# Neighbourhood attention in an encoder: left and right key blocks folded into one before exp and transposes, scores three steps ahead, bias table built in other places

## The chip, the cores and the metric

The kernel runs on one core of a Trainium2 chip. The metric is the device time of one execution in microseconds (us). Times of runs are medians of several executions; a trace is one profiled execution, which has a time of its own. PE is the matrix engine (TensorE), PEld its weight loads, DVE VectorE, ACT ScalarE, POOL GpSimd, SP the engine whose queue issues the DMAs here.

## What is computed

The program is an encoder of two layers on 1024 tokens (a grid of 16 rows by 64 columns) of width 1024, in fp32. Layer 0 has mixer A, attention of 16 heads of width 64 over a window of 8 rows by 16 columns; layer 1 has mixer B, attention over all keys. Each is followed by an output projection and a gated embedding. The change touches mixer A alone:

```python
rs = np.clip(r - win_r // 2, 0, rows - win_r)
cs = np.clip(c - win_c // 2, 0, GRID_W - win_c)
...
sc = jnp.einsum('bhqd,bhqnd->bhqn', qb, kg).astype(jnp.float32) * scale
sc = sc + bb.astype(jnp.float32)[None]
pr = jax.nn.softmax(sc, axis=-1).astype(vg.dtype)
return jnp.einsum('bhqn,bhqnd->bhqd', pr, vg)
```

`bb` is a learned bias for each head and each row and column offset. The result is multiplied by silu(gate) and projected.

## The kernel before

**Tiles.** The tokens are put in another order first: each of the 8 tiles of 128 tokens holds all 16 rows of 8 neighbouring columns. A window of 16 columns then lies in a query's own tile and the two beside it (`near(j)`), so a query block j has scores for 3 key blocks (2 at the edges, j = 0 and 7). Of the left block a query at column c of its tile sees the keys with column at least c, of the right block those with column below c; the two sets complement each other. A mask of a large number (`MK`) takes out the rest.

**Number format.** Matmuls take every fp32 operand as a high part (an ACT copy in fp32r) and a low part (a DVE subtraction of it), so a product is 2 or 3 matmuls on line 303.

**A step.** The loop runs over 16 heads h and 8 blocks j, 128 steps n. With the sign of the scores turned, step (h, j) issues, in the order of the code:

- `head`: due work of the list `later` (among it `fin`, the gating of a finished pair of heads), and at j = 1 `table(h + 1)`: one DMA of the next head's bias (`u`, line 609, SP) and five POOL subtractions of 128x128 (line 612) that make `tb` = mask minus bias.
- `f_T(h, j)`: one PE transpose for each key block (line 654), then the ACT copy PTh (657) and the DVE subtraction PTl (658). There are two PSUM buffers `t`.
- `f_E` of step n + 1: ACT's exp (646) over all blocks, with the row's minimum `mn` as bias, and row sums.
- `f_S` of step n + 2: two matmuls into `s`, then one DVE instruction (637) that adds `tb`, writes `sp` to SBUF and takes the minimum. `sp` and `mn` have three buffers.
- `f_AV` of step n - 2: the products with V, key block by key block, from PTh and PTl.

**Dense work.** `mix` spreads matmuls of the projections (q and k of head h + 1, gates, for h = 3, 7, 11 also V of the next four heads) between these pieces in proportion to weights. Every fourth head, 3, 7 and 11, therefore takes longer. Each engine executes its instructions in the order in which they were issued, one queue for each.

**The end of a pair of heads.** `head_end` (line 418) sends reciprocals of the row sums over DRAM by SP (`r8T` to `rD`, line 436, `rD` to `rb`, 438). `fin`, four ticks later, has two POOL products of 128x512, Y by G (499) and Y by rb (500). Eleven pulses later ACT makes the high part (496, written to `rb`), DVE the low part (497), and SP stores both (492).

**Weights.** They come through a staging buffer (`wstage`, SP) and are split by ACT and DVE (lines 218 and 219) between the other work. q and k of a head are split on DVE by lines 588, 589, 590 and 593, four times two for each head.

Of the kernel before, what the change touches and what calls it, by code (L numbers as in the profile page):

```python
# [11 lines left out]
F32 = mybir.dt.float32  # L12
F32R = mybir.dt.float32r
# [70 lines left out]
def lay_out(inp):  # L84
# [46 lines left out]
    ok = np.stack([rowok, left, rowok, right, rowok], axis=1)  # L131
    mask = np.where(ok, 0.0, BIG).astype(np.float32)

    inv = np.power(np.float32(10000.0), -np.arange(16, dtype=np.float32) * np.float32(2.0) / np.float32(32.0)).astype(np.float32)
# [7 lines left out]
    def swap(v):  # L142
# [5 lines left out]
        "x": tokens(g["x"][0]), "wts": W, "rpb": rpb, "gains": gains, "hgains": hg,  # L148
        "mask": mask, "rope": np.stack([cosT, sinT], axis=1),
    }  # L150


@with_exitstack
def trunk(ctx, tc, x, wts, rpb, gains, hgains, mask, rope, out):
    nc = tc.nc
# [384 lines left out]
    def mixer_a():  # L540
        with ExitStack() as es:
# [64 lines left out]

            def table(h):
                u = sb.tile([128, 16, 24], F32, name="u", bufs=1)
                sync.dma_start(u, U2[h].rearrange("p (r c) -> p r c", r=16))
                tb = sb.tile([128, 640], F32, name="tb").rearrange("p (k c) -> p k c", k=5)  # L610
                for k, c0 in ((0, 0), (1, 0), (2, 8), (3, 16), (4, 16)):
# [3 lines left out]
                TB[h] = tb  # L615

# [3 lines left out]
            def f_S(h, j):  # L620
                k0, k1 = near(j)
                n = (k1 - k0 + 1) * 128
                ps = psS.tile([128, 512], F32, name="s")
                qt = QS[h][:, j * 128:(j + 1) * 128]
                ks = slice(k0 * 128, (k1 + 1) * 128)
                mm(ps[:, :n], qt, KA[h][:, ks], True, False)
                mm(ps[:, :n], qt, KB[h][:, ks], False, True)
                if j == 0:
                    RS[h] = sb.tile([128, 8], F32, name="rs", bufs=3)
                    tb = TB[h][:, 2:5:2]  # L630
                elif j == NT - 1:
                    tb = TB[h][:, 0:3:2]
                else:
                    tb = TB[h][:, 1:4]
# [12 lines left out]

            def f_T(h, j):
                k0, k1 = near(j)
                m = k1 - k0 + 1  # L650
                sp, _ = SP.pop((h, j))
                ps = psT.tile([128, 4, 128], F32, name="t")
                for i in range(m):
                    pe.transpose(ps[:, i], sp[:, i * 128:(i + 1) * 128], ident)  # L654
                f0 = k0 * 3 + (j - k0 + 1)
                sl = slice(f0, f0 + 2 * m - 1, 2)
# [6 lines left out]
            def f_AV(h, kb):  # L663
# [3 lines left out]
                for hf in range(2):  # L667
                    a, b = max(j0, 4 * hf), min(j1, 4 * hf + 3)
                    if a > b:
                        continue  # L670
                    first = OP[h][hf] is None
                    if first:
                        OP[h][hf] = psO.tile([128, 512], F32, name="o")
                    o = OP[h][hf][:, (a - 4 * hf) * 128:(b + 1 - 4 * hf) * 128]
                    s0 = kb * 3 + a - kb + 1
                    sl = slice(s0, s0 + b - a + 1)
                    last = kb == (4 if hf == 0 else 7)
                    mm(o, V[:, kb, h % 4], PTh[:, sl], first, False)
                    mm(o, V[:, kb, h % 4], PTl[:, sl], False, last)
# [65 lines left out]
            vs[0][1]()  # L745
            sync.dma_start(MK, mask)
            for c in range(8):
                sync.dma_start(U[:, c], rpb[:, :, 7 - c:31 - c])
            for t in range(1, NT):
# [8 lines left out]
                vs[t][1]()  # L758
                if t == 6:
                    table(0)  # L760
                WQ.pump(t > 2)
# [7 lines left out]
            ptp = es.enter_context(tc.tile_pool(name="ptp", bufs=1))  # L769
            PTh = ptp.tile([128, NT * 3, 128], F32R, name="PTh")  # L770
            PTl = ptp.tile([128, NT * 3, 128], F32R, name="PTl")
            for d in qk_items(0):
# [9 lines left out]
            f_E(0, 0)  # L782
            f_S(0, 1)
            steps = [(h, j) for h in range(NH) for j in range(NT)]

# [6 lines left out]
            for h in range(NH):  # L792
                att = []
                for j in range(NT):
                    n = h * NT + j
                    def head(h=h, j=j):
                        later.tick()
                        if j == 1 and h + 1 < NH:
                            table(h + 1)
                    att.append((head, CA[0]))  # L800
                    att.append((lambda h=h, j=j: f_T(h, j), CA[1]))
                    if n + 1 < len(steps):
                        att.append((lambda n=n: f_E(*steps[n + 1]), CA[2]))
# [9 lines left out]
                if h == NH - 1:  # L813
                    att += [(lambda: f_AV(NH - 1, NT - 2), CA[4]), (lambda: f_AV(NH - 1, NT - 1), CA[4])]
                dense = []
# [469 lines left out]

NAMES = ["x", "wts", "rpb", "gains", "hgains", "mask", "rope"]

# [14 lines left out]
```

## Time and profile before

| what | value |
| --- | --- |
| median of 3 runs | 1562.63 us (1560.91 to 1562.86) |
| the profiled execution | 1564.6 us |
| span of its trace | 1562.8 us |
| PE busy, whole span | 1520.8 us (97%) |
| DVE, ACT, POOL busy | 965.3, 871.6 and 320.3 us |
| mixer A, 60 to 545 us of the trace: PE, DVE, ACT, POOL busy | 476.11, 298.78, 282.17 and 77.67 us |

The span is the trace's own measure; the 1.8 us between it and the time of the execution lie outside it. An engine's busy time is summed over instructions; on PE, matmuls overlap, so that one instruction's duration is longer than the distance from its start to that of the next.

### The profile page before, as it was taken

To read this page: it belongs to the slowest core of one execution; us is meant where nothing else is said; L and a number is where in the kernel's file an instruction comes from. 1 tells how busy PE (TensorE), PEld (TensorE's weight loads), DVE (VectorE), ACT (ScalarE), POOL (GpSimd) and SP (SyncE) were. 2 spreads that over 40 slices of the span, in tenths; PEclk is the share of its full clock that TensorE was granted. 3 is DMA by queue.
4 is the path that set the end of the run, shared out by engine and by line. 5 is a ranking of instruction groups with operands and counts; after the bars stand their busy time and mean duration, and the time that the engine had idled before them with its cause. 6 is when DMAs were issued, how large, how long until landed. Compare 5 with 4: busy or idle time off the path is not lost.

```text
span 1562.8 us, 23940 instructions
## 1 busy us (share of the span) xinstructions
PE 1520.8 (97%) x9048; PEld 1328.0 (85%) x9048; DVE 965.3 (62%) x1660; ACT 871.6 (56%) x1744; POOL 320.3 (20%) x409
## 2 busy tenths in 40 slices
PE   6999999999999999999999999999999999999998
PEld 6888988988988788888988889989899888778886
DVE  5566576476467434536767776677777777624533
ACT  6565465466366523433566776776767777622422
POOL 3102102112012010000433142553141400000124
PEclk9999999999999999999999999999999999999999
DMA  8211222132122962132210111101101213651113
GB/s 288 83 40 53 66 67 78 40 93 79 40 80 83 340 237 90 53 130 104 77 49 22 38 51 42 59 24 55 50 27 46 77 39 107 233 202 54 68 59 130
DMA packets 89859, 138.82 MB, mean 89 GB/s; under 512 B 16913, under 2 KB 55953, under 8 KB 89745
## 3 DMA queue, kind: packets, MB, share of 16 engines
q1 hardware_dynamic: 85136, 122.62, 23.9%
q10 hardware_dynamic: 4608, 14.68, 2.6%
q8 instruction: 71, 1.16, 0.3%
q14 instruction: 44, 0.35, 0.1%
HBM read 104.65 MB, written 36.15 MB: 90 GB/s over the span
## 4 chain that ended last, share of the span: by engine, by line
PE 81%; ACT 6%; DVE 6%; issue 3%; POOL 2%; DMA 2%; SPq 0%; ACTq 0%; POOLq 0%; DVEq 0%
PE d L303 54%; PE o L303 10%; PE s L303 8%; PE t L1057 6%; PE t L654 2%; DVE PTl L1060 2%; PE t L413 2%; DVE mn L1041 1%; DMA wstage<-in_wts 1%; ACT PTh L1059 1%; ACT wh L218 1%; ACT P L1047 1%; POOL xn L402 1%; DVE wl L219 1%; POOL tb L612 1%
## 5 line engine op out<-in xcount | busy, mean ns | idle before, releaser
L303 PE MATMUL d<-wh,HTh 128*128 128x256 f32 (+1 forms) x1096 | 372.3, 340 | 4.9 <-ACT HTh L414 2.6
L303 PE MATMUL d<-wh,HTl 128*128 128x256 f32 (+1 forms) x1096 | 365.7, 334 | 1.5 <-DVE HTl L415 1.5
L303 PE MATMUL d<-wl,HTh 128*128 128x256 f32 (+1 forms) x1096 | 365.2, 333 | 0.0
L1060 DVE TENSOR_TENSOR PTl<-t,PTh 128x512 fp32r<-128x512 f32 x256 | 164.4, 684 | 123.4 <-ACT PTh L1059 122.8
L303 PEld LDWEIGHTS d<-wh,HTh 128*128 128x128 f32 x1096 | 207.7, 189 | 28.4 <-ACT HTh L414 3.2
L303 PEld LDWEIGHTS d<-wh,HTl 128*128 128x128 f32 x1096 | 207.7, 189 | 23.8 <-DVE HTl L415 2.1
L303 PEld LDWEIGHTS d<-wl,HTh 128*128 128x128 f32 x1096 | 208.0, 190 | 21.4
L303 PE MATMUL d<-HTh,wh 128*128 128x512 f32 x504 | 206.1, 409 | 0.0
L303 PE MATMUL d<-HTl,wh 128*128 128x512 f32 x504 | 197.7, 392 | 0.0
L303 PE MATMUL d<-HTh,wl 128*128 128x512 f32 x504 | 197.7, 392 | 0.0
L1047 ACT ACTIVATE P<-s,mn 128x1024 f32<-128x1024 f32 x128 | 142.8, 1115 | 58.3 <-DVE mn L1041 57.7
L1059 ACT ACTIVATE PTh<-t 128x512 fp32r<-128x512 f32 x256 | 139.9, 594 | 43.2 <-PE t L1057 42.3
L1041 DVE TENSOR_REDUCE mn<-s 128x1 f32<-128x1024 f32 x128 | 154.7, 1209 | 11.7 <-PE s L303 11.5
L1057 PE MATMUL t<-ident,P 128*128 128x128 f32 x1024 | 137.4, 275 | 6.7 <-DVE PTl L1060 4.8
L219 DVE TENSOR_TENSOR wl<-wstage,wh 128x1024 fp32r<-128x1024 f32 x89 | 113.8, 1284 | 39.9 <-ACT wh L218 39.4
L1057 PEld LDWEIGHTS t<-ident,P 128*128 128x128 f32 x1024 | 114.7, 141 | 22.5 <-DVE PTl L1060 16.5
L303 PE MATMUL s<-KA,QS 128*128 128x512 f32 (+2 forms) x384 | 133.7, 402 | 0.0
L303 PE MATMUL o<-PTh,V 128*128 128x256 f32 (+2 forms) x672 | 119.0, 288 | 3.3 <-ACT PTh L657 1.7
L303 PE MATMUL s<-KB,QS 128*128 128x512 f32 (+2 forms) x384 | 121.8, 371 | 0.0
L303 PE MATMUL o<-PTl,V 128*128 128x256 f32 (+2 forms) x672 | 119.5, 289 | 0.4 <-DVE PTl L658 0.3
L658 DVE TENSOR_TENSOR PTl<-t,PTh 128x384 fp32r<-128x384 f32 (+1 forms) x128 | 66.6, 520 | 79.3 <-ACT PTh L657 78.3
L303 PEld LDWEIGHTS d<-HTh,wl 128*128 128x128 f32 x504 | 94.6, 188 | 22.0
(159 smaller groups left out, 2456.7 us busy)
## 6 DMA issues: line engine op xcount, KB each, us to landing
wstage<-in_wts SPq DMA_DIRECT2D x92, 512.0 KB
X<-in_x SPq DMA_DIRECT2D x16, 512.0 KB
pp<-ppD SPq DMA_DIRECT2D x32, 256.0 KB
rb<-rD SPq DMA_DIRECT2D x56, 128.0 KB
ppD<-th SPq DMA_DIRECT2D x24, 256.0 KB
xD<-X SPq DMA_DIRECT2D x8, 512.0 KB
X<-xD SPq DMA_DIRECT2D x8, 512.0 KB
yD0h<-rb SPq DMA_DIRECT2D x14, 256.0 KB
```

Source lines behind the costliest of these rows:

```text
L218: act.activation(hi, s, AF.Copy)
L219: self.rest = lambda: dve.tensor_tensor(lo, s, hi, ALU.subtract)
L303: pe.matmul(ps, a, b, start=first, stop=last, skip_group_check=True)
L402: pool.tensor_scalar(xns[i][:, :512], xts[i][:, :512], r[:, i:i + 1], None, op0=ALU.mult)
L413: pe.transpose(ps[:, k], xn[:, (4 * c + k) * 128:(4 * c + k + 1) * 128], ident)
L654: pe.transpose(ps[:, i], sp[:, i * 128:(i + 1) * 128], ident)
L658: dve.tensor_tensor(PTl[:, sl], ps[:, :m], PTh[:, sl], ALU.subtract)
L1041: dve.tensor_reduce(mn, ps, axis=AX.X, op=ALU.min)
L1047: act.activation(p, ps, AF.Exp, bias=mn, scale=-1.0, accum_out=RS[h, hf][:, t:t + 1])
L1057: pe.transpose(ps[:, i], p[:, k * 128:(k + 1) * 128], ident)
L1059: act.activation(PTh[:, ks, c], ps, AF.Copy)
L1060: dve.tensor_tensor(PTl[:, ks, c], ps, PTh[:, ks, c], ALU.subtract)
```

## The change

Before, a step has 3 blocks at exp and at the transposes. After, DVE takes the element-wise minimum of the left and the right block behind the wide score instruction (for j = 1 to 6, so 6 times for each of 16 heads, 96 in all), and exp, transposes, PTh and PTl handle 2 blocks. Since each element is masked in one of the two blocks, the minimum is the one that isn't. Behind the transposes two POOL instructions of 128x2x128 pull the two apart again with a mask RI: right = folded by RI, left = folded minus right. PTh and PTl are now the two halves of one tile PT. The scores are still computed at 3 blocks, and the products with V are the same in number and width.

The scores run three steps ahead (four buffers of `sp` and `mn`), the products with V three steps behind. The bias of head h + 1 is fetched at j = 0, and its table is built at j = 2 (two blocks) and j = 3 (three), where all of it stood at j = 1. For head 0 the opening loop over tiles fetches the bias at t = 5 and builds the table at t = 7, where both stood at t = 6. The mask RI is a new input of 64 KB, loaded once behind MK.

```diff
+            RI = one.tile([128, 128], F32, name="RI")
...
-            def table(h):
+            def bias(h):
                 u = sb.tile([128, 16, 24], F32, name="u", bufs=1)
                 sync.dma_start(u, U2[h].rearrange("p (r c) -> p r c", r=16))
...
+            def table(h, ks):
...
-                sp = sb.tile([128, 384], F32, name="sp", bufs=3)
-                mn = sb.tile([128, 1], F32, name="mn", bufs=3)
+                sp = sb.tile([128, 384], F32, name="sp", bufs=4)
+                mn = sb.tile([128, 1], F32, name="mn", bufs=4)
...
+                if n == 384:
+                    dve.tensor_tensor(sp[:, 0:128], sp[:, 0:128], sp[:, 256:384], ALU.min)
...
                 n = (k1 - k0 + 1) * 128
+                n = min(n, 256)
                 sp, mn = SP[h, j]
...
-                for i in range(m):
+                for i in range(2):
                     pe.transpose(ps[:, i], sp[:, i * 128:(i + 1) * 128], ident)
...
-                act.activation(PTh[:, sl], ps[:, :m], AF.Copy)
-                dve.tensor_tensor(PTl[:, sl], ps[:, :m], PTh[:, sl], ALU.subtract)
+                act.activation(PT[:, 0, sl], ps[:, :2], AF.Copy)
+                dve.tensor_tensor(PT[:, 1, sl], ps[:, :2], PT[:, 0, sl], ALU.subtract)
+                if m == 3:
+                    left, right = PT[:, :, f0], PT[:, :, f0 + 4]
+                    pool.tensor_tensor(right, left, RI[:, None].to_broadcast([128, 2, 128]), ALU.mult)
+                    pool.tensor_tensor(left, left, right, ALU.subtract)
...
-                        if j == 1 and h + 1 < NH:
-                            table(h + 1)
+                        if h + 1 < NH:
+                            if j == 0:
+                                bias(h + 1)
+                            elif j == 2:
+                                table(h + 1, (2, 4))
+                            elif j == 3:
+                                table(h + 1, (0, 1, 3))
...
-                    if n + 2 < len(steps):
-                        att.append((lambda n=n: f_S(*steps[n + 2]), CA[3]))
-                    if n >= 2:
-                        att += av_and_v(*steps[n - 2])
+                    if n + 3 < len(steps):
+                        att.append((lambda n=n: f_S(*steps[n + 3]), CA[3]))
+                    if n >= 3:
+                        att += av_and_v(*steps[n - 3])
```

In the changed kernel the lines that the next listings name have these numbers: 620 is the table's subtraction, 500 and 501 are the products Y by G and Y by rb, 672 and 673 the two that pull the blocks apart; on ACT 657 is exp, 668 the copy PT, 497 the high part of Y, 583, 586 and 587 the copies of a projection of q and k, 219 the high part of weights; on SP 611 is the bias, 204 the staging of weights, 437 and 439 the two legs of the row sums.

**POOL, around the first finished pair (head 2).** Before:

```order
L612 TENSOR_TENSOR tb<-MK,u 128x128 x20
L499 TENSOR_TENSOR Y<-Y,G 128x512
L500 TENSOR_TENSOR Y<-Y,rb 128x512
L499 TENSOR_TENSOR Y<-Y,G 128x512
L500 TENSOR_TENSOR Y<-Y,rb 128x512
L612 TENSOR_TENSOR tb<-MK,u 128x128 x10
```

After:

```order
L620 TENSOR_TENSOR tb<-MK,u 128x128 x2
L672 TENSOR_TENSOR PT<-PT,RI 128x2x128
L673 TENSOR_TENSOR PT<-PT 128x2x128
L500 TENSOR_TENSOR Y<-Y,G 128x512
L501 TENSOR_TENSOR Y<-Y,rb 128x512
L620 TENSOR_TENSOR tb<-MK,u 128x128 x3
```

The table of head 3 stood whole ahead of the first pair's two products; now two of its five blocks and a step's pulling apart stand ahead of them, and the other three behind.

**ACT, head 2, around the high part of that pair's Y.** Before:

```order
L584 ACTIVATE QS<-th 64x512
L585 ACTIVATE KA<-th 64x512
L657 ACTIVATE PTh<-t 128x3x128
L646 ACTIVATE sp,rs<-sp,mn 128x384
L496 ACTIVATE rb<-Y 128x512
L657 ACTIVATE PTh<-t 128x3x128
L646 ACTIVATE sp,rs<-sp,mn 128x384
```

After:

```order
L657 ACTIVATE sp,rs<-sp,mn 128x256
L583 ACTIVATE th<-d 128x512
L219 ACTIVATE wh_1358<-wstage 128x1024
L497 ACTIVATE rb<-Y 128x512
L586 ACTIVATE QS<-th 64x512
L587 ACTIVATE KA<-th 64x512
L668 ACTIVATE PT<-t 128x2x128
```

The high part of Y stood ahead of the copy of step (2, 4) and now stands one step later, ahead of the copy of step (2, 5).

**SP, head 2.** Before:

```order
L436 DMA rD<-r8T 8x32 x4
L438 DMA rb<-rD 64x512 x2
L203 DMA wstage<-in_wts 128x1024
L609 DMA u<-U_84 128x384
L436 DMA rD<-r8T 8x32 x4
```

After:

```order
L611 DMA u<-U_84 128x384
L204 DMA wstage<-in_wts 128x1024
L437 DMA rD<-r8T 8x32 x4
L439 DMA rb<-rD 64x512 x2
L437 DMA rD<-r8T 8x32 x4
```

The bias of head 3 stood behind the first pair's first row sums and a weight tile and now stands ahead of both.

## Rows read from the trace of the kernel before

**Rows 1.** The page, busy time of each engine over the whole span (share, instructions):

```profile
PE 1520.8 (97%) x9048; PEld 1328.0 (85%) x9048; DVE 965.3 (62%) x1660; ACT 871.6 (56%) x1744; POOL 320.3 (20%) x409
```

**Rows 2.** Windows: length, busy PE, PEld, DVE, ACT, POOL (instructions), clock, DMA share, GB/s:

```profile
60.00:545.00 485.00, 476.11 (x2704) 414.08 (x2704) 298.78 (x675) 282.17 (x626) 77.67 (x103) 1.00 0.27 88
...
84.24:134.85 50.61, 49.32 (x262) 41.89 (x262) 36.21 (x85) 32.69 (x73) 8.79 (x9) 1.00 0.21 68
```

**Rows 3.** Timeline of PE: start, duration, line, operation; three transposes, then a step with two:

```profile
96.22 0.39 PE L303 MATMUL d<-HTh,wl 128*128 128x512 f32 x1
96.45 0.49 PE L654 MATMUL t<-ident,sp 128*128 128x128 f32 x3
...
96.95 0.34 PE L303 MATMUL s<-KB,QS 128*128 128x384 f32 x1
...
134.85 0.38 PE L654 MATMUL t<-ident,sp 128*128 128x128 f32 x2
...
135.24 0.34 PE L303 MATMUL s<-KB,QS 128*128 128x384 f32 x1
```

**Rows 4.** Groups by form, mixer A: count | busy us, mean ns of one | idle before:

```profile
L654 PE MATMUL t<-ident,sp 128*128 128x128 f32 x352 | 60.4, 275 | 6.0 <-ACT sp L646 5.6
L646 ACT ACTIVATE sp<-sp,mn 128x384 f32<-128x384 f32 x96 | 58.9, 614 | 11.1 <-DVE mn L637 10.5
L658 DVE TENSOR_TENSOR PTl<-t,PTh 128x384 fp32r<-128x384 f32 x96 | 53.4, 556 | 66.2 <-ACT PTh L657 65.3
L657 ACT ACTIVATE PTh<-t 128x384 fp32r<-128x384 f32 x96 | 47.1, 490 | 51.0 <-PE t L654 49.6 <-issue 0.8
L588 DVE SCALAR_TENSOR_TENSOR QS<-th,QS 64x512 fp32r<-64x512 f32 x32 | 23.4, 731 | 7.2 <-ACT QS L584 6.3
L646 ACT ACTIVATE sp<-sp,mn 128x256 f32<-128x256 f32 x32 | 16.2, 505 | 2.8 <-DVE mn L637 2.8
L658 DVE TENSOR_TENSOR PTl<-t,PTh 128x256 fp32r<-128x256 f32 x32 | 13.2, 412 | 13.1 <-ACT PTh L657 13.0
L657 ACT ACTIVATE PTh<-t 128x256 fp32r<-128x256 f32 x32 | 12.3, 383 | 11.3 <-PE t L654 10.5
```

**Rows 5.** Groups by form, mixer B: SBUF operations of two inputs on POOL and DVE:

```profile
L878 POOL TENSOR_TENSOR qt<-qt,t 128x256 f32<-128x256 f32 x24 | 19.4, 807 | 1.9
...
L878 DVE TENSOR_TENSOR qt<-qt,t 128x128 f32<-128x128 f32 x8 | 2.4, 302 | 0.3
```

**Rows 6.** Waits: who waited on whom, total us, times, median us:

```profile
ACT rb L496 <- POOL Y L500: 11.8, 3, 4.3
...
PE t L654 <- ACT sp L646: 5.6, 6, 1.5
```

**Rows 7.** Timeline, SP, POOL, ACT and PE in heads 2 and 14:

```profile
113.10 0.37 SPq L609 DMA_DIRECT2D u<-U  x1
...
117.14 3.06 POOL L612 TENSOR_TENSOR tb<-MK,u 128x128 f32<-128x128 f32 x5 [35.14 <-DMA u<-U]
...
123.17 0.63 ACT L496 ACTIVATE rb<-Y 128x512 fp32r<-128x512 f32 x1 [4.10 <-POOL Y L500]
...
124.83 0.55 PE L654 MATMUL t<-ident,sp 128*128 128x128 f32 x3 [1.29 <-ACT sp L646]
...
492.58 0.61 ACT L646 ACTIVATE sp<-sp,mn 128x384 f32<-128x384 f32 x1 [3.46 <-DVE mn L637]
...
493.34 0.55 PE L654 MATMUL t<-ident,sp 128*128 128x128 f32 x3 [1.27 <-ACT sp L646]
```

**Rows 8.** Two DVE lines, ns min/median/max, first to last start:

```profile
L588 DVE SCALAR_TENSOR_TENSOR QS<-th,QS x32: 684/686/1787, 53.1 to 496.9; 64x512 fp32r<-64x512 f32 x32
...
L637 DVE CUSTOM_DVE_ANT_0 sp<-s,tb x96: 506/548/559, 60.8 to 525.3; 128x384 f32<-128x384 f32 x96
```

**Rows 9.** Timeline, head 4, PE and POOL:

```profile
197.20 0.49 PE L654 MATMUL t<-ident,sp 128*128 128x128 f32 x3
...
199.61 1.40 POOL L500 TENSOR_TENSOR Y<-Y,rb 128x512 f32<-128x512 f32 x1 [8.53 <-DMA rb<-rD]
```

More of the change, by code (lines that the diff above doesn't have):

```diff
@@ L132, in lay_out @@
     mask = np.where(ok, 0.0, BIG).astype(np.float32)
+    side = (c[:, None] < c[None, :]).astype(np.float32)
     inv = np.power(np.float32(10000.0), -np.arange(16, dtype=np.float32) * np.float32(2.0) / np.float32(32.0)).astype(np.float32)
@@ L148, in lay_out, with trunk @@
         "x": tokens(g["x"][0]), "wts": W, "rpb": rpb, "gains": gains, "hgains": hg,
-        "mask": mask, "rope": np.stack([cosT, sinT], axis=1),
+        "mask": mask, "side": side, "rope": np.stack([cosT, sinT], axis=1),
     }
 @with_exitstack
-def trunk(ctx, tc, x, wts, rpb, gains, hgains, mask, rope, out):
+def trunk(ctx, tc, x, wts, rpb, gains, hgains, mask, side, rope, out):
     nc = tc.nc
@@ L605, in qk_items @@
                 return it
-            def table(h):
+            def bias(h):
                 u = sb.tile([128, 16, 24], F32, name="u", bufs=1)
                 sync.dma_start(u, U2[h].rearrange("p (r c) -> p r c", r=16))
-                tb = sb.tile([128, 640], F32, name="tb").rearrange("p (k c) -> p k c", k=5)
-                for k, c0 in ((0, 0), (1, 0), (2, 8), (3, 16), (4, 16)):
+                TB[h] = (None, u)
+            def table(h, ks):
+                tb, u = TB[h]
+                if tb is None:
+                    tb = sb.tile([128, 640], F32, name="tb").rearrange("p (k c) -> p k c", k=5)
+                for k in ks:
+                    c0 = (0, 0, 8, 16, 16)[k]
                     pool.tensor_tensor(tb[:, k].rearrange("p (r c) -> p r c", r=16),
@@ L614, in table @@
                                        u[:, :, c0:c0 + 8], ALU.subtract)
-                TB[h] = tb
+                TB[h] = (tb, u)
             def near(j):
@@ L629, in f_S @@
                     RS[h] = sb.tile([128, 8], F32, name="rs", bufs=3)
-                    tb = TB[h][:, 2:5:2]
+                    tb = TB[h][0][:, 2:5:2]
                 elif j == NT - 1:
-                    tb = TB[h][:, 0:3:2]
+                    tb = TB[h][0][:, 0:3:2]
                 else:
-                    tb = TB[h][:, 1:4]
-                sp = sb.tile([128, 384], F32, name="sp", bufs=3)
-                mn = sb.tile([128, 1], F32, name="mn", bufs=3)
+                    tb = TB[h][0][:, 1:4]
+                sp = sb.tile([128, 384], F32, name="sp", bufs=4)
+                mn = sb.tile([128, 1], F32, name="mn", bufs=4)
                 dve.tensor_tensor_reduce(out=sp[:, :n].rearrange("p (k c) -> p k c", c=128),
@@ L652, in f_T @@
                 ps = psT.tile([128, 4, 128], F32, name="t")
-                for i in range(m):
+                for i in range(2):
                     pe.transpose(ps[:, i], sp[:, i * 128:(i + 1) * 128], ident)
                 f0 = k0 * 3 + (j - k0 + 1)
-                sl = slice(f0, f0 + 2 * m - 1, 2)
-                act.activation(PTh[:, sl], ps[:, :m], AF.Copy)
-                dve.tensor_tensor(PTl[:, sl], ps[:, :m], PTh[:, sl], ALU.subtract)
+                sl = slice(f0, f0 + 3, 2)
+                act.activation(PT[:, 0, sl], ps[:, :2], AF.Copy)
[4 more added lines that the diff above has]
+                    pool.tensor_tensor(left, left, right, ALU.subtract)
             def talloc():
@@ L677, in f_AV @@
                     last = kb == (4 if hf == 0 else 7)
-                    mm(o, V[:, kb, h % 4], PTh[:, sl], first, False)
-                    mm(o, V[:, kb, h % 4], PTl[:, sl], False, last)
+                    mm(o, V[:, kb, h % 4], PT[:, 0, sl], first, False)
+                    mm(o, V[:, kb, h % 4], PT[:, 1, sl], False, last)
                     if last:
@@ L746, in mixer_a @@
             sync.dma_start(MK, mask)
+            sync.dma_start(RI, side)
             for c in range(8):
@@ L758, in mixer_a @@
                 vs[t][1]()
-                if t == 6:
-                    table(0)
+                if t == 5:
+                    bias(0)
+                if t == 7:
+                    table(0, range(5))
                 WQ.pump(t > 2)
@@ L769, in mixer_a @@
             ptp = es.enter_context(tc.tile_pool(name="ptp", bufs=1))
-            PTh = ptp.tile([128, NT * 3, 128], F32R, name="PTh")
-            PTl = ptp.tile([128, NT * 3, 128], F32R, name="PTl")
+            PT = ptp.tile([128, 2, NT * 3, 128], F32R, name="PT")
             for d in qk_items(0):
@@ L783, in mixer_a @@
             f_S(0, 1)
+            f_S(0, 2)
             steps = [(h, j) for h in range(NH) for j in range(NT)]
@@ L813, in mixer_a @@
                 if h == NH - 1:
-                    att += [(lambda: f_AV(NH - 1, NT - 2), CA[4]), (lambda: f_AV(NH - 1, NT - 1), CA[4])]
+                    att += [(lambda kb=kb: f_AV(NH - 1, kb), CA[4]) for kb in range(NT - 3, NT)]
                 dense = []
@@ L1283, in trunk @@
     dense_phase(1)
-NAMES = ["x", "wts", "rpb", "gains", "hgains", "mask", "rope"]
+NAMES = ["x", "wts", "rpb", "gains", "hgains", "mask", "side", "rope"]
 def kernel(**inputs):
```

## The prediction

> **What bounds the kernel now.** First the page's busy times: PE works 1520.8 of 1562.8 us, every other engine at most 62% [rows 1]. Then the windows, because only mixer A is touched: from 60 to 545 us PE is busy 476.11 of 485.00 us and POOL 77.67 [rows 2]. So the stretch is bound by PE, and an edit pays in two ways only: by work that leaves PE, or by what is left of 8.9 us in which PE stands still. Next the timeline of PE, for what one instruction really costs: not its duration but the distance to the next start. Last the waits of PE and, one step behind them, of the engine that PE waited for: six waits of the transposes for exp, 5.6 us together, and three waits of ACT's Y copy for POOL, 11.8 us [rows 6]. ACT's and DVE's long idle times behind exp and copies [rows 4] cost nothing; PE works meanwhile.
>
> **Fewer transposes.** Three transposes and the first score matmul behind them take from 96.45 to 96.95, 0.50 us; with two it is 134.85 to 135.24, 0.39 us [rows 3]. The score matmuls are 384 wide in both steps, so the difference of 0.11 us is one transpose. Of the 352 transposes, 96 go: 96 x 0.11 = 10.6 us of PE's own path. The duration in the group's row is 275 ns [rows 4], but the instructions overlap: a wide matmul of 0.39 us is followed by the next start 0.23 us later (96.22 to 96.45) [rows 3]. The score matmuls and the products with V are the same in number and width, so nothing else leaves PE.
>
> The Trainium skill ("TensorE: Matmul & The Clock Gate", Part 4: PE-mode transpose) gives about 275 ns for a transpose inside a kernel. The duration here agrees to the nanosecond, but the starts lie 0.11 us apart; by the page's figure the term would be 96 x 0.275 = 26.4 us.
>
> **Cheaper exp, copies and subtractions.** From 384 to 256 columns exp falls from 614 to 505 ns, the copy from 490 to 383, the subtraction from 556 to 412 [rows 4]. ACT loses 96 x (0.109 + 0.107) = 20.7 us, DVE 96 x 0.144 = 13.8. I count nothing for this: PE's transposes wait for exp only 5.6 us in six places [rows 6], and those have another cause (below).
>
> **The minimum on DVE, the pulling apart on POOL.** The minimum takes two SBUF inputs of 128x128; the like on DVE took 302 ns [rows 5], so DVE gets 96 x 0.30 = 29 us, and 313.8 in all of about 471. A POOL instruction of two inputs of 128x256 took 807 ns [rows 5]; 192 of them are 155 us, so POOL goes from 78 to 233 us, half of the stretch. Neither is on PE's path by itself. The minimum stands between score and exp, but the scores now run a step further ahead: a step lasts 50.61 / 16 = 3.2 us [rows 2], and 0.3 us more is well covered. The pulling apart stands between the transposes and the products with V. Those now come three steps behind and need the pulling apart of the step two before: some 2.6 steps, 8.2 us, after its transposes start. Its own chain is transposes 0.38, copy 0.38, subtraction 0.41 and two POOL instructions 1.61, 2.8 us, with handoffs estimated at up to 0.9; at least 4.5 us are spare. Without that cover each wide step would cost its 1.6 us: 96 x 1.6 = 154 us. So the price is 0 now, and what could use up the 4.5 us is a rival.
>
> **The bias and the table.** In head 2 the bias was issued at 113.10, POOL could begin the table only at 117.14 and took 3.06 us; the two products with the finished pair stood behind it in POOL's order. ACT, in order as well, sat at the high part of Y for 4.10 us until 123.17, exp of the next step stood behind that, and the transposes began 1.29 us late at 124.83 [rows 7]. Heads 6 and 10 show the same (transposes at 247.02 and 370.08): the three waits of ACT sum to 11.8 us [rows 6], and PE's part of them is 3.3 us of idle. Idle is counted from the end of the matmul before, of whose 0.39 us 0.16 overlaps otherwise with the next; so 3.3 + 3 x 0.16 = 3.8 us are lost. After the change the bias goes out at j = 0, ahead of row sums and weight tile, two of five table blocks stand ahead of the two products instead of five, and ACT's copy of Y stands a step later. The bias DMA delays the queue behind it by its 0.37 us issue [rows 7]; the row sums have a step more. POOL now has a pulling apart (1.6 us) ahead of the products, but no wait for the DMA, and less table by three fifths of 3.06 us, 1.8. So ACT finds Y done, by about a step: all 3.8 us count as gained. From both sides: at worst nothing is gained (the wait is replaced), at best 3.8.
>
> **What isn't counted.** The fourth late transpose, at 493.34, lost 1.27 + 0.16 = 1.4 us: exp waited 3.46 us for the score's minimum on DVE [rows 7], while POOL and DVE were busy at once. Three steps of lead help it, more POOL work harms it: 0, with 1.4 on either side. At the start, one more score matmul pair stands ahead of the loop, at the end three products with V instead of two; both shift PE's waits there but add no PE work: 0, with 1.5 us on either side. The two DMAs (RI, 64 KB, and the bias of head 0 a tile sooner) lie in the opening, where PE waits for neither: 0.
>
> **Sum.** 10.6 + 3.8 = 14.4 us. The span would go from 1562.8 to 1548.4, the profiled execution from 1564.6 to 1550.2. That one lies 2.0 above the median of the runs, 1562.63; from the median the forecast is 1548.2 us. A change of 0.2%, 3.1 us, is about what can be told from none.
>
> **Rivals.**
>
> Only the transposes count: POOL's new work ahead of the two products of a pair makes ACT wait as long as the bias did. For: POOL is three times as busy. Against: the room of about a step. 1562.6 - 10.6 = 1552.0 us.
>
> All of PE's idle time goes: 10.6 + 8.9 = 19.5, 1543.1 us. For: three steps of lead everywhere. Against: a part of it is the start and the end, where no lead can be built up.
>
> DVE and POOL block each other. Where POOL is at work, DVE's line 588, with its two inputs in SBUF, took up to 1787 instead of 686 ns; line 637, which reads the scores in PSUM and one input in SBUF, never took over 559 [rows 8]. In heads 1 and 2 DVE is busy 36.21 of 50.61 us [rows 2]; with twelve minima less twelve cheaper subtractions, 38.1, of 50.61 - 12 x 0.11 - 1.45 = 47.8. There are twelve minima and some 24 others that read only SBUF (sixteen of lines 588 to 593, eight of 219, 497 and 513). DVE becomes the bound when each of the 36 loses (47.8 - 38.1) / 36 = 0.27 us, and over six such pairs of heads, 216 instructions, the gain is used up at 0.27 + 14.4 / 216 = 0.34 us. The measured mean loss of line 588 is 731 - 686 = 45 ns [rows 4, 8], with POOL busy 8.79 of 50.61, 17%; with 24 x 0.81 = 19.4 us more it is 59%, so by proportion 0.15 us: DVE at 43.5 of 47.8, 91%. Close, but under. If each lost half a POOL instruction, 0.40, the sum would be 0.13 x 216 = 28 us against the gain: 1576 us, slower; if each lost a whole one, 0.81, 0.54 x 216 = 117 us: 1665 us.
>
> The Trainium skill ("SBUF — State Buffer", Who interferes with whom) says that DVE with two SBUF inputs and a GpSimd instruction reading SBUF exclude each other, and that the one that comes second waits in full. Lines 588 and 637 agree with it, 1787 ns against 559 at most. By that rule, with every one of the 36 second, it would be the last of these times.
>
> POOL, in order, is held by a DMA. In head 4 POOL sat 8.53 us at the product Y by rb, until 199.61 [rows 9], and three more such waits of about 7 to 9 us stand in mixer A. Now pullings apart stand behind that product. If the whole wait came on top, each place would cost 8.53 + 1.40 - 4.5 = 5.4 us, four of them 21.7: 1570 us, slower; from 14.4 / 4 = 3.6 us each it decides. Against: in the new order POOL reaches the product only behind the pulling apart of step (4, 5), whose transposes stood at 197.20 [rows 9]; that ends 2.8 us later, Y by G takes POOL to about 201.4, and rb landed at 199.6, a step later by the products' longer lag at most 202.8. A wait of 1.4 us is left, under the 4.5.
>
> A transpose is worth its whole duration of 275 ns [rows 4]: 96 x 0.275 = 26.4, 1536.2 us. The start times speak against it [rows 3].
>
> **How the numbers follow.** Forecast 0.56; only the transposes 0.18; all idle time 0.08; DVE and POOL blocking 0.11 (0.02 with a part of the gain left, 0.05 at no change, 0.04 slower); POOL held 0.05; whole duration 0.02. Likeliest: 1548.2 us. The range reaches from the case of no idle time, less a microsecond for its end, to the blocking at 0.31 us for each instruction (0.04 x 216 = 8.6 us, about 1557) with a microsecond more: 1542 to 1558. Left out are 0.02 and 0.05 + 0.04 + 0.05, with half of the 0.02: about 0.17. Faster 0.86, same 0.05, slower 0.09.
>
> **What would show it.** In the changed profile 256 transposes, two of them and the next start 0.39 us apart; no ACT wait for POOL at the high part of Y; POOL near 230 us in mixer A, DVE near 320 to 370; PE's waits for exp below 2 us. Wrong would be: PE waiting in the products with V for POOL (held or overloaded), transposes waiting for exp behind the minimum (DVE late), or DVE at over 95% in the heads without V work. More than 20 us gained would mean that a transpose is worth more than 0.11 us.

## Result and the profile after

The changed kernel takes 1569.42 us (median of 5 runs, 1567.75 to 1570.83), the one before 1562.65 (5 runs). The ratio is 1.0044, 95% interval 1.0029 to 1.0059: slower by 6.8 us, where 14.4 us less were forecast. The traced execution of the changed kernel took 1567.75 us, its span is 1566.0, 3.2 us more than the 1562.8 of before. So the trace shows about half of the difference of the medians: it is the fastest of its five runs, and the traced one of before lay 2 us above its median. The granted clock of the five runs of the changed kernel lies between 0.993 and 0.996, and the two at 0.993 are the two slowest (1570.64 and 1570.83 us); the traced execution of before had 0.997.

The page's busy times and, from the windows, mixer A (columns as in [rows 2]):

```profile
PE 1514.3 (97%) x8952; PEld 1319.0 (84%) x8952; DVE 1026.7 (66%) x1756; ACT 850.0 (54%) x1744; POOL 491.7 (31%) x601
```

```profile
60.00:545.00 485.00, 469.36 (x2608) 405.42 (x2609) 359.52 (x769) 258.67 (x624) 248.79 (x295) 0.99 0.26 84
```

Against [rows 1, 2], PE has 96 instructions less and is busy 6.7 us less in mixer A: the work did leave PE. But the stretch didn't get shorter, so PE stands still longer. POOL went from 77.67 to 248.79 us, DVE from 298.78 to 359.52. At the 302 ns that the prediction took for a minimum, the minima less the cheaper subtractions explain 15 of DVE's 61 us; the rest is instructions taking longer, the minima (387 ns) among them. The groups of the changed kernel (lines 590, 591 and 592 were 588, 589 and 590; 665 is the transposes, 668 and 669 copy and subtraction, 649 the minimum):

```profile
L672 POOL TENSOR_TENSOR PT<-PT,RI 128x256 fp32r<-128x256 f32 x96 | 80.2, 835 | 237.6 <-DVE PT L669 205.8 <-issue 31.9
L649 DVE TENSOR_TENSOR sp<-sp 128x128 f32<-128x128 f32 x96 | 37.2, 387 | 3.3
L591 DVE TENSOR_TENSOR KB<-th,KA 64x512 fp32r<-64x512 f32 x32 | 36.4, 1136 | 0.5
L590 DVE SCALAR_TENSOR_TENSOR QS<-th,QS 64x512 fp32r<-64x512 f32 x32 | 31.6, 988 | 7.2 <-ACT QS L586 6.3
L592 DVE CAST KA<-KA 64x512 fp32r<-64x512 f32 x32 | 28.1, 879 | 0.8
```

Line 588 of before had 731 ns [rows 4]; now it is 988. The waits of the changed kernel (who waited on whom, total us, times, longest us), to be set against [rows 6]:

```profile
ACT wh L219 <- DMA wstage<-in_wts: 11.5, 6, 4.7
PE t L665 <- ACT sp L657: 10.2, 8, 2.3
...
PE s L304 <- DVE mn L645: 5.6, 3, 3.5
ACT rb L497 <- POOL Y L501: 2.7, 3, 1.3
```

The wait that the new places of bias and table were to remove is gone: ACT on POOL, 11.8 us before, 2.7 now. In its place transposes wait 10.2 us for exp (5.6 before), and score matmuls 5.6 us for DVE, which they never did. PE's timeline shows where. First the start of mixer A:

```profile
57.35 0.33 PE L304 MATMUL s<-KB,QS 128*128 128x384 f32 x1
61.15 0.69 PE L304 MATMUL s<-KA,QS 128*128 128x384 f32 x1 [3.46 <-DVE mn L645]
61.63 0.52 PE L304 MATMUL s<-KB,QS 128*128 128x384 f32 x1
61.95 0.63 PE L304 MATMUL d<-HTh,wh 128*128 128x512 f32 x1
62.38 0.63 PE L304 MATMUL d<-HTl,wh 128*128 128x512 f32 x1
...
71.00 0.38 PE L665 MATMUL t<-ident,sp 128*128 128x128 f32 x2
```

There are two PSUM buffers for scores. The third score pair, (0, 2), now issued ahead of the loop, waits until DVE has read the first, and PE, in order, waits with it, with dense matmuls queued behind. After this wait the dense matmuls take 0.63 us and start 0.43 apart (0.39 and 0.23 in [rows 3]): PE is at 1.2 GHz for ten of them and part of an eleventh (granted clock 0.50 from 61.9 to 66.6 us), then at 2.4 again (1.00). The first transposes come at 71.00; before they came at 64.12:

```profile
64.12 0.38 PE L654 MATMUL t<-ident,sp 128*128 128x128 f32 x2
```

Then the head after each head with V work (here head 4), chain from DVE to PE on four engines:

```profile
194.89 1.68 DVE L591 TENSOR_TENSOR KB<-th,KA 64x512 fp32r<-64x512 f32 x1
...
196.60 1.41 DVE L592 CAST KA<-KA 64x512 fp32r<-64x512 f32 x1
...
199.24 1.23 DVE L220 TENSOR_TENSOR wl<-wstage,wh 128x1024 fp32r<-128x1024 f32 x1
...
200.49 1.86 SPq L204 DMA_DIRECT2D wstage<-in_wts  x2
...
203.97 1.06 ACT L219 ACTIVATE wh<-wstage 128x1024 fp32r<-128x1024 f32 x1 [1.54 <-DMA wstage<-in_wts]
...
204.93 0.62 ACT L497 ACTIVATE rb<-Y 128x512 fp32r<-128x512 f32 x1
...
206.73 0.39 ACT L668 ACTIVATE PT<-t 128x256 fp32r<-128x256 f32 x1
...
207.14 0.51 ACT L657 ACTIVATE sp<-sp,mn 128x256 f32<-128x256 f32 x1
...
207.80 0.44 PE L665 MATMUL t<-ident,sp 128*128 128x128 f32 x2 [2.01 <-ACT sp L657]
```

DVE frees the weights' staging buffer (line 220) late, behind two lengthened q and k instructions; the next DMA goes out only then, and ACT, in order, sits at the high part of that weight tile with exp behind it. The same stands at 330.66 and 451.93 (2.01 and 1.98 us of idle); behind the last of them PE ran six matmuls at the lower clock (granted clock 0.50 from 452.7 to 455.1 us). Last the scores of step (3, 3):

```profile
136.40 1.14 DVE L591 TENSOR_TENSOR KB<-th,KA 64x512 fp32r<-64x512 f32 x1
...
137.57 1.41 DVE L592 CAST KA<-KA 64x512 fp32r<-64x512 f32 x1
...
139.46 0.94 DVE L595 CAST KB<-KB 64x512 fp32r<-64x512 f32 x1
...
140.43 0.56 DVE L645 CUSTOM_DVE_ANT_0 sp<-s,tb 128x384 f32<-128x384 f32 x1
...
141.05 0.44 PE L304 MATMUL s<-KA,QS 128*128 128x384 f32 x1 [1.07 <-DVE mn L645]
```

From 131 to 141 us DVE is busy 9.80 of 10 us and POOL 8.07 (windows):

```profile
131.00:141.00 10.00, 8.82 (x46) 7.00 (x45) 9.80 (x17) 5.85 (x15) 8.07 (x7) 1.00 0.51 146
```

Where the trace's difference comes from, from the start times on PE in the two traces (a start's excess over its usual distance from the one before):

| what | us |
| --- | --- |
| 96 transposes less | -10.6 |
| the four late transposes of before (124.83, 247.02, 370.08, 493.34) gone | -5.2 |
| wait for the score buffer at 61.15, and the lower clock behind it | +6.2 |
| three waits in head 0 (2.8 us, before 1.6) | +1.2 |
| transposes (4, 6), (8, 6), (12, 6): 6.5 us and 1.2 of lower clock, before 0.8 | +6.9 |
| scores (3, 3), (7, 3) and four small waits beside them | +3.7 |
| sum | +2.2 |
| measured | +3.2 |

A start's excess is the idle time of the timeline plus 0.16 us, by which the matmul before would have overlapped. The waits at the very end of mixer A, about 5 us, stand in both traces and are left out.

### The profile page after: what moved, and what is told of

The parts are those of the page before. It is cut to its first block, busy times and chain, and to the rows that moved or that the text cites. A ratio compares the mean times of both kernels' runs of the same rounds, so it can differ in the third digit from the quotient of the medians.

```text
span 1566.0 us, 24148 instructions
## 1 busy us (share of the span) xinstructions
PE 1514.3 (97%) x8952; PEld 1319.0 (84%) x8952; DVE 1026.7 (66%) x1756; ACT 850.0 (54%) x1744; POOL 491.7 (31%) x601
## 3 DMA queue, kind: packets, MB, share of 16 engines
q8 instruction: 71, 1.16, 0.3%
## 4 chain that ended last, share of the span: by engine, by line
PE 77%; DVE 7%; ACT 5%; issue 5%; DMA 3%; POOL 2%; SPq 0%; ACTq 0%; POOLq 0%; DVEq 0%
PE d L304 51%; PE o L304 10%; PE s L304 8%; PE t L1080 6%; DMA wstage<-in_wts 2%; PE t L414 2%; DVE PTl L1083 2%; PE t L665 1%; DVE mn L1064 1%; DVE wl L220 1%; ACT PTh L1082 1%; ACT P L1070 1%; ACT wh L219 1%; POOL xn L403 1%; PE t L1034 0%
## 5 line engine op out<-in xcount | busy, mean ns | idle before, releaser
L672 POOL TENSOR_TENSOR PT<-PT,RI 128x256 fp32r<-128x256 f32 x96 | 80.2, 835 | 237.6 <-DVE PT L669 205.8
L312 POOL TENSOR_TENSOR stn<-stn,neghalf 128x2 f32<-128x2 f32 (+1 forms) x20 | 12.9, 646 | 325.7 <-DVE stn L398 325.7
L304 PEld LDWEIGHTS d<-HTh,wh 128*128 128x128 f32 x504 | 95.7, 190 | 13.4 <-ACT G L509 0.2
```

Source lines behind the costliest of these rows:

```text
L304: pe.matmul(ps, a, b, start=first, stop=last, skip_group_check=True)
L672: pool.tensor_tensor(right, left, RI[:, None].to_broadcast([128, 2, 128]), ALU.mult)
```

## Experiments

All times are medians; the kernel before, run beside them, took 1562.1 to 1562.75 us.

**e1, the third score late.**

```diff
-            f_S(0, 2)
...
-                        att.append((lambda n=n: f_S(*steps[n + 3]), CA[3]))
+                        att.append((lambda n=n: [f_S(*steps[i]) for i in range(n + 3 if n else 2, n + 4)], CA[3]))
```

> The changed kernel, but the scores of step (0, 2) are issued in step (0, 0), next to those of (0, 3), and no longer ahead of the loop; nothing else is moved. Theory A (the third score pair ahead of the loop waits for one of two PSUM buffers s, holds PE for 3.6 us, and PE then runs at the lower clock for some 4 us): PE's wait at 61 us goes, the loop starts 6 to 7 us sooner, 1562 to 1564 us where the changed kernel takes 1569.4. Rival (head 0 waits anyway, for exp or for the pulling apart): the wait moves to the first steps of head 0 and less than 3 us is gained, 1567 or more.

1563.77 us (11 runs, 1561.4 to 1565.89; ratio to before 1.0006, 0.9997 to 1.0014): 5.6 us less than the changed kernel. In its trace the loop starts 6.2 us sooner and no matmul there is at the lower clock:

```profile
57.76 0.34 PE L304 MATMUL s<-KB,QS 128*128 128x384 f32 x1
64.76 0.38 PE L665 MATMUL t<-ident,sp 128*128 128x128 f32 x2
```

Theory A holds. What is left is no gain over the kernel before, with all the later waits still there.

**e2, no pulling apart.**

```diff
-                    pool.tensor_tensor(right, left, RI[:, None].to_broadcast([128, 2, 128]), ALU.mult)
-                    pool.tensor_tensor(left, left, right, ALU.subtract)
...
+            pool.memset(PT.bitcast(F32), 0.0)
```

> The changed kernel without the two POOL instructions that pull the folded block apart; the right blocks of PT are zero all the time, so part of the computation is left out. All orders and lags stay. Theory B (POOL's instructions lengthen those of DVE that read two inputs, or copy, in SBUF; DVE comes late with weights and scores): lines 591 and 592 of the changed kernel go back from 1136 and 879 ns to about 690 and 420, the five waits of PE at about 140, 206, 263, 329 and 450 us go, 9 to 11 us are gained, 1558 to 1561. Rival C (order and lags alone make them): the waits stay, at most 2 us are gained, 1567 to 1569.

1557.13 us (0.9964, 0.9950 to 0.9977), 12.3 less than the changed kernel, a little more than theory B said. Lines 591 and 592 are back at 690 and 485 ns:

```profile
L591 DVE TENSOR_TENSOR KB<-th,KA 64x512 fp32r<-64x512 f32 x32 | 22.1, 690 | 0.5
L592 DVE CAST KA<-KA 64x512 fp32r<-64x512 f32 x32 | 15.5, 485 | 0.8
```

The transposes after the V heads come 0.8 to 1.0 us late instead of 2.2, and the scores of (3, 3) and (7, 3) no longer wait. The chain in head 4 shows it: the weight DMA goes out 2.75 us ahead of the transposes of (4, 5) (196.05 and 198.80), in the changed kernel 1.50 (200.49 and 201.99), and ACT doesn't wait for it:

```profile
196.05 2.63 SPq L204 DMA_DIRECT2D wstage<-in_wts  x2
...
199.36 1.06 ACT L219 ACTIVATE wh<-wstage 128x1024 fp32r<-128x1024 f32 x1
...
203.19 0.44 PE L665 MATMUL t<-ident,sp 128*128 128x128 f32 x2 [0.63 <-ACT sp L657]
```

Six late transposes stay in heads 2 to 12 (0.6 to 1.0 us each); e3 has them too, so they belong to order and lags. C falls as the main cause.

**e3, the lags and table places without the fold.**

```diff
-                if n == 384:
-                    dve.tensor_tensor(sp[:, 0:128], sp[:, 0:128], sp[:, 256:384], ALU.min)
...
-                n = min(n, 256)
...
-                for i in range(2):
+                for i in range(m):
```

> The lags, the buffers and the places of bias and table as in the changed kernel, but no fold: three blocks through exp, transposes and copies, no minimum, no pulling apart. Theory B: the start loses 7 us as in the changed kernel, the four old waits of 5.2 us go, and no new one comes: 1563 to 1566. Rival C: the waits after the heads with V (206, 329, 450 us in the changed kernel) and at the score of (3, 3) and (7, 3) are there too, another 10 us: 1573 to 1576.

(Copies three blocks wide, no pulling apart.) 1567.45 us (1.0032, 1.0020 to 1.0044), a little over B's range. The start's loss is there in full (a wait of 3.6 us at 62 and eleven matmuls at the lower clock), the four old waits are gone, but six new ones of 0.7 to 0.9 us stand in heads 2, 4, 6, 8, 10 and 12: with the start's 5.6 us set aside, 1561.8 us are left, 0.9 under the kernel before, which the intervals don't tell from none.

**e4, a third transpose.**

```diff
+                if m == 3:
+                    pe.transpose(ps[:, 2], sp[:, 256:384], ident)
```

> The changed kernel with a third transpose in each of the 96 wide steps, of the block that the minimum has already taken in; its output isn't read. If a transpose is worth 0.11 us of PE's path: 10.6 us more, 1578 to 1581. If PE's waits take it up: less than 5 us more. If it is worth its duration of 0.275 us: 26 us more, 1595.

1572.63 us, 3.2 more. Each transpose does add 0.11 us of PE work; but the later PE comes, the less it waits: the waits after the V heads shrink from 2.2 to 1.8 us, the one of 2.5 near the end to 0.6, the six matmuls behind 451.93 run at full clock, and behind the wait at the start seven, not ten, at the lower one. In the changed kernel PE comes to places where DVE and ACT are late, and there most of what fewer transposes save goes into waiting.

**e7, two transposes in the kernel before.**

```diff
-                for i in range(m):
+                for i in range(2):
...
+                src = ps[:, :2] if m == 2 else ps[:, 0:1].to_broadcast([128, 3, 128])
```

> The kernel before, with two transposes in place of three in the wide steps; copies and subtractions stay three blocks wide and read the first block three times, so the third block is left out of the computation. It prices the first term alone. If a transpose is 0.11 us of the path and the waits stay: 1551 to 1553. If PE's waits take up a part (as the third transpose in e4 cost 3 us and not 10.6): 1555 to 1559.

1554.57 us (0.9956, 0.9943 to 0.9969), 7.5 less than before by the medians; the interval allows 5 to 9, not the 10.6 of the start times. The spans differ by 10.4 (1552.4 against 1562.8), but the traced execution of before lay 2 us above its median. The result lies between the two ranges expected, nearer to the second. In e7's trace nine transposes wait for exp, six before, 5.1 us together against 5.6; where the missing 3 us went was not followed.

**e5, the q and k copies on ACT** (on top of e1).

```diff
-                        dve.tensor_copy(ka[lo, s], ka[hi, s])
+                        act.activation(ka[lo, s], ka[hi, s], AF.Copy)
...
-                        dve.tensor_copy(kb[lo, s], kb[hi, s])
+                        act.activation(kb[lo, s], kb[hi, s], AF.Copy)
```

> The changed kernel with the third score late (as in e1), and with the two copies in the splitting of q and k (lines 592 and 595, SBUF to SBUF, 879 and 625 ns on DVE in the changed kernel) on ACT. Theory B (DVE, lengthened by POOL, is late): DVE loses 48 us of work, the waits of PE at 135, 202, 257, 325 and 447 us of e1 shrink, 1557 to 1560 us against 1563.8 of e1. Rival D (ACT's own order is what makes the transposes late, since exp stands behind weight and q/k copies): 64 more ACT instructions of some 0.63 us in that order make the waits longer, 1564 to 1572.

1569.39 us, 5.6 more than e1: rival D. DVE is busy 44 us less than in the changed kernel, and the scores' waits vanish, but exp is late instead:

```profile
PE t L665 <- ACT sp L657: 20.5, 22, 2.6
```

**e6, the scores two ahead.**

```diff
-            f_S(0, 2)
...
-                    if n + 3 < len(steps):
-                        att.append((lambda n=n: f_S(*steps[n + 3]), CA[3]))
+                    if n + 2 < len(steps):
+                        att.append((lambda n=n: f_S(*steps[n + 2]), CA[3]))
```

> The changed kernel with the scores two steps ahead as in the kernel before, all else as changed (products with V three behind). The wait at the start goes as in e1. If the third step of lead is what covers a late DVE: exp and with it the transposes wait more often, 1566 to 1572. If the lead only moved the waits to the score matmuls (which wait for a PSUM buffer at 135 and 257 us of e1): 1560 to 1563.

1573.7 us, 9.9 more than e1, where the start is the same, and a little over the range: the third step of lead does cover a late DVE. Without it exp waits 32.9 us for the minimum on DVE, and the transposes wait for exp in 25 places:

```profile
ACT sp L657 <- DVE sp L649: 32.9, 25, 3.2
PE t L665 <- ACT sp L657: 22.4, 25, 2.2
```

**e8, the fold with the old lags and the old place of the table.**

```diff
-                            if j == 0:
-                                bias(h + 1)
...
+                        if h + 1 < NH and j == 1:
+                            bias(h + 1)
+                            table(h + 1, range(5))
...
-                        att.append((lambda n=n: f_S(*steps[n + 3]), CA[3]))
-                    if n >= 3:
-                        att += av_and_v(*steps[n - 3])
+                        att.append((lambda n=n: f_S(*steps[n + 2]), CA[3]))
+                    if n >= 2:
+                        att += av_and_v(*steps[n - 2])
```

> The fold (minimum, two blocks, pulling apart) with everything else as before: scores two ahead, products with V two behind, bias and table at j = 1. With 8.2 us between transposes and products shortened by a step of 3.2, POOL's pulling apart is covered by about 1 us only. Theory B: PE waits in the products with V for POOL wherever POOL has other work or is lengthened, several times in each pair of heads, 1570 to 1600. Rival E (the lags buy nothing): 1560 to 1564.

1595.24 us (1.0211, 1.0197 to 1.0226). The products wait for the pulling apart in 30 places. The four longest, at 126.37 and its like in heads 6, 10 and 14, make 16.1 of the 35.2 us: POOL, in order, sat at the table until the bias had landed, with a step's pulling apart behind it.

```profile
PE o L304 <- POOL PT L673: 35.2, 30, 4.6
```

```profile
121.70 2.62 POOL L620 TENSOR_TENSOR tb<-MK,u 128x128 f32<-128x128 f32 x5 [9.84 <-DMA u<-U]
124.28 1.17 POOL L672 TENSOR_TENSOR PT<-PT,RI 128x256 fp32r<-128x256 f32 x1
125.53 0.79 POOL L673 TENSOR_TENSOR PT<-PT 128x256 fp32r<-128x256 f32 x1
...
126.37 0.79 PE L304 MATMUL o<-PT,V 128*128 128x256 f32 x2 [4.59 <-POOL PT L673]
```

**e9, POOL's load alone, in the kernel before.**

```diff
+                if m == 3:
+                    for _ in range(2):
+                        pool.tensor_tensor(JK, PTl[:, f0:f0 + 3:2].bitcast(F32), MK[:, 0:2], ALU.mult)
```

> The kernel before, unchanged in its own work, with two more POOL products of 128x256 behind the low part of each of the 96 wide steps; their result is read by nobody, so nothing waits for them but what stands behind them in POOL's order, and DVE where the two exclude each other. It prices POOL's load alone. Theory B: line 588 goes from 731 to about 950 ns, the transposes wait more often for exp, 4 to 12 us more, 1566 to 1574. If the load alone harms nothing (the harm is in waits for the pulling apart): 1562 to 1564, with DVE's durations longer or not.

1574.69 us (1.0077, 1.0064 to 1.0089). The size is B's, but not the way: most of the loss stands in three places where ACT waits for the gating of Y in POOL's order, now up to 6.3 us, and PE up to 3.48 us, each with six matmuls at the lower clock behind. That is 6.8 us of wait more than before and 3.6 of lower clock, of 12.5.

```profile
ACT rb L496 <- POOL Y L500: 23.9, 10, 6.3
```

So e9 couldn't tell DVE's lengthening from POOL's queue. e13 was made for that.

**e13, POOL loaded, but writing only.**

```diff
-                    pool.tensor_tensor(right, left, RI[:, None].to_broadcast([128, 2, 128]), ALU.mult)
-                    pool.tensor_tensor(left, left, right, ALU.subtract)
+                    for f in (f0, f0 + 4):
+                        for _ in range(3):
+                            pool.memset(PT[:, :, f].bitcast(F32), 0.0)
```

> The changed kernel with the two pulling-apart instructions of a step replaced by six POOL instructions that only write zeros, three on the left and three on the right slot, at the same place in POOL's order, behind the same low part and with the same products waiting for them; the folded block's values are lost, so that part of the computation is left out. POOL stays loaded and awaited but reads nothing from SBUF there. Theory B (POOL's reads and DVE's second input exclude each other): DVE's lines 591 and 592 fall from 1136 and 879 ns to about 700 and 480, PE's waits at 140, 206, 263, 329 and 450 us shrink, and the time is within 2 us of e2, 1556 to 1560. Rival G (POOL's load and order, or the products' wait for it, make the loss whatever it reads): as the changed kernel, 1566 to 1570, with DVE's durations short or not.

1557.58 us (0.9967, 0.9954 to 0.9979), as e2. POOL is as busy as in the changed kernel (253.42 against 248.79 us), stands in the same order, and the products still depend on it; the reads of the pulling apart are gone. DVE's instructions with two inputs are short again, and the transposes of (4, 6) wait less than half as long as the 2.01 us at 207.80:

```profile
60.00:545.00 485.00, 474.90 (x2652) 411.88 (x2653) 327.75 (x777) 262.78 (x629) 253.42 (x679) 1.00 0.28 89
```

```profile
L592 DVE CAST KA<-KA 64x512 fp32r<-64x512 f32 x32 | 23.1, 722 | 0.8
L590 DVE SCALAR_TENSOR_TENSOR QS<-th,QS 64x512 fp32r<-64x512 f32 x32 | 22.1, 692 | 7.2 <-ACT QS L586 6.3
L591 DVE TENSOR_TENSOR KB<-th,KA 64x512 fp32r<-64x512 f32 x32 | 22.1, 689 | 0.5
```

```profile
203.60 0.44 PE L665 MATMUL t<-ident,sp 128*128 128x128 f32 x2 [0.95 <-ACT sp L657]
```

B holds for the instructions with two inputs, G falls. The copy on line 592 does not fall to 480 ns as expected, but stays at 722. That also weighs against the rival that the zeros are harmless because they are short (321 ns each, the pulling apart 835 and 858): beside short ones a copy does lengthen, yet 590 and 591 do not.

**e14, e1 and e2 together.**

```diff
-            f_S(0, 2)
...
-                    pool.tensor_tensor(right, left, RI[:, None].to_broadcast([128, 2, 128]), ALU.mult)
-                    pool.tensor_tensor(left, left, right, ALU.subtract)
```

> e1 and e2 together: the third score late and no pulling apart (right blocks are zero, part of the computation is left out). If the start (5.6 us in e1) and the pulling apart (12.3 us in e2) are separate losses that explain the change between them: 1569.4 - 5.6 - 12.3 = 1551.5, 1549 to 1553, three us or so above the forecast. If they overlap: 1555 to 1557.

1552.75 us (0.9935, 0.9923 to 0.9947; span 1548.7). The two losses add up: 16.7 us of the 17.9 that they measure apart. The forecast was 1548.2; of the 21.2 us between it and the changed kernel, start and pulling apart are 16.7.

**e10, e11, e12, is there more to be had?** All on top of e1: weight tiles split later, the same with Y's parts later, and Y's parts later alone.

```diff
+            WQ.age = AGE + 6
...
-YS = (11, 11)
+YS = (13, 11)
```

> e1 (the third score late), and in mixer A a weight tile is split nine pulses after its staging at the soonest, not three; so ACT takes it up behind exp and no longer sits in front of it until the DMA has landed. Theory F (in e1 PE's waits at 202, 325 and 447 us, 2.1 to 2.3 each, and the one of 2.4 at 531 are ACT waiting for a weight DMA that came late because DVE freed the staging buffer late): they shrink to under 1 us, 5 to 8 us less than e1, 1556 to 1559. Rival: ACT's queue stays late through its other work there (high part of Y, copies of q and k), or PE waits for weights instead: 1562 to 1566.

> e10, and in mixer A the high and low part of Y stand 13 pulses behind the gating, not 11, so that ACT's copy of it comes behind exp instead of ahead. If ACT's order is what is left: 1 to 3 us less than e10. If DVE's load is: the same as e10 within 1 us.

> e1 with the Y parts two pulses later and the weights as they were. If the clump of copies on ACT ahead of exp makes the three waits of 2.1 to 2.3 us: each loses 0.6, 1.5 to 3 us less than e1, 1561 to 1562.5. If the weight DMA alone sets them: as e1, 1563.8.

e10 (`WQ.age` alone) takes 1558.49 us (0.9979, 0.9970 to 0.9989): it beats both kernels, the one before by 3.6 us. ACT no longer waits at the weights in head 4, and the transposes of (4, 6) come without a wait, where e1 has 1.93 us; a wait of 0.79 for DVE stands two steps on, at (5, 0). So the chain from the staging buffer to exp is what made them late. e12 (`YS` alone) takes 1559.41 (0.9983), more gain than expected; both together 1561.86 (1.0000), against the expectation. In e11 the transposes and scores wait for DVE (4.2 and 4.4 us) and several stretches are at the lower clock. Why the two don't add up was not followed further.

## Why the prediction was wrong

**Fewer transposes: right on PE's path, too large in time.** e7 gives 7.5 us by the medians for the 10.6 of the sum. What failed is the silent assumption that PE stays the bound everywhere: with new lateness in DVE and ACT, which PE has to wait for, the third transposes cost only 3.2 us when they are put back (e4).

**Bias and table: right by its mechanism.** ACT's wait for POOL fell from 11.8 to 2.7 us and the late transposes are gone. But e3 shows six smaller waits in their stead, so of the 3.8 us that were counted, lags and table together leave about 0.9, which is not clear of noise.

**"What isn't counted": the step that failed first.** The one more score pair ahead of the loop was put at 0, with 1.5 us on either side, as a shift of PE's waits. It cost 6.2 us in the trace, 5.6 in the medians (e1). The working counted its matmuls and not its buffer: two PSUM buffers for scores, three scores issued before anything reads one, and the first reader behind q and k's splitting in DVE's order. Nor did it count the clock behind a wait of 3.5 us.

**"DVE and POOL block each other": named, and put aside by the wrong test.** The mechanism is the one of that rival, shown by e13: 12 us. Its size was nearly right on average: 0.15 us was taken for each instruction, and the lines that lengthen (220, 498, 590 to 595, 649) lose 49 us against e2 in 274 instructions, 0.18 each. Single lines were sized low: 590 loses 0.30, 591 0.45 us, the minimum 0.02. (The 43.5 us of that working count the loss of 0.045, which the measured 36.21 held already, a second time.) But the step that failed is the point from which it decides, 0.27 us, where DVE would be full over two heads. DVE never was: it is busy 359.52 of 485 us, 74%. The instructions that lengthen stand together, the splitting of q and k beside a weight tile and a pair's Y, and there DVE is full for ten microseconds, though the stretch has room. From such a place the lateness goes on by a chain that no busy share shows: staging buffer, DMA, ACT's order, exp.

The Trainium skill ("SBUF — State Buffer", Who interferes with whom) says that a DVE instruction with two SBUF inputs contends with a GpSimd one that reads SBUF, not with one that only writes. e13 agrees: lines 590 and 591 are at 692 and 689 ns while POOL writes, 988 and 1136 while it reads.

**The cover of the products: right.** One wait of 1.16 us for POOL in the products at 84.69 and nothing like the rival's four places of 3.6; e8 shows what the third step of lag and the early bias are for. The cover was thinner than worked out, though: from the start of a wide step's transposes to the end of its pulling apart the changed kernel's trace has 5.0 us in the median and up to 8.6, where the working had 2.8 to 3.7 of 8.2.

**What stays open.** The medians differ by 6.8 us, the traces by 3.2; the trace's account says nothing about the other 3.6. That stretches of lower clock make them was seen in no trace; only the granted clocks of the runs point that way. Of the 21.2 us of error, e14 leaves 4.5. Two terms of the sum bear on them: the six late transposes that e3 brought, which stand in e14's trace too (4.4 us together), and the transposes' gain, 3 us short in e7. No run separates the two.

## What to carry to other kernels

An edit that issues work earlier takes a buffer earlier: count the buffers of each tile that it fills, and who must have read the first before the next can be issued. Judge an engine that slows down not by its share over a stretch but in the microseconds in which its lengthened instructions stand together, and follow from there what it frees: a staging buffer freed 1.2 us later than in e2 reached TensorE by a DMA and another engine's queue, as 1.4 us more of waiting. Work moved to GpSimd is not free because GpSimd is idle; where it reads SBUF beside VectorE instructions with two SBUF inputs, both pay (line 591 690 to 1136 ns; GpSimd's table subtraction, line 620, 506 to 592, e2 against the changed kernel).

## What the runs showed of the hardware

Copies on DVE with one SBUF input (line 592) lengthen even where POOL only writes: 722 ns in e13, 485 in e2 without the pulling apart, 879 where POOL reads; line 595 has 625, 460 and 625. The prediction had counted them with the others; they behave differently. The Trainium skill (the same page and section) has copies able to run in a mode with two ports that contends with GpSimd, and makes no exception there for a GpSimd that only writes. The three numbers agree; that line 592 ran in that mode no run shows.

In the changed kernel a wait of PE of 3.46 us was followed by ten matmuls at 1.2 GHz (0.63 us each, 0.43 apart), one of 1.98 at 451.93 by six, and two of 2.01 at 207.80 and 330.66 by none. The same wait of 3.46 us was followed by seven in e2 and e4 and by six in e13.
